# One RWKV-7 layer with a gated ConvFFN: own buffers for the first raw weight block of each seven-product pair, stores and half of the sum of squares off GpSimd

## The chip, the cores and the metric

The kernel runs on one core of a Trainium2 chip. The metric is the device time of one execution in microseconds (us). Engines are named as the profile names them: PE is TensorE (PEld its weight loads), DVE VectorE, ACT ScalarE, POOL GpSimd, SP the engine that issues most of the DMAs (SPq in the rows).

## The reference, cut to what matters

One layer on 512 tokens (T) of width D = 2048, all float32: an RWKV-7 time mixer, then a ConvFFN with 5504 hidden channels; each between two RMS norms and scaled by a conditioning vector. What the change touches is the residual between the two halves, and the ConvFFN's up-projection:

```
def _rms(x, g):
    y = xf * lax.rsqrt(jnp.mean(xf * xf, axis=-1, keepdims=True) + RMS_EPS)
    return (y * g).astype(x.dtype)
def _conv_ffn(h, w_in, conv_w, conv_b, w_out):
    u = _causal_dwconv(h @ w_in, conv_w, conv_b)
    gate, val = jnp.split(u, 2, axis=-1)
    return (jax.nn.silu(gate) * val) @ w_out
...
        x = x + g_m * _rms(y, norm_mix_post[layer])
        h = _rms(x, norm_ffn_pre[layer]) * (1 + sc_f) + sh_f
        f = _conv_ffn(h, ffn_w_in[layer], ffn_conv_w[layer], ffn_conv_b[layer], ffn_w_out[layer])
```

Each output of `_rms` needs the sum of squares over all 2048 channels of a token before it can be scaled.

## The kernel before, in words

Channels lie on the 128 partitions, tokens along the free axis; KT = 16 blocks of channels make up D, FT = 43 blocks the hidden width. Float32 accuracy comes from three products of rounded parts: a weight tile is split into wh (rounded, a cast on ACT, L220, L1314, L1304) and wl (the remainder, a subtraction on DVE, L222, L1315, L1305), the activations into xh and xl, and PE adds wh·xh + wh·xl + wl·xh. So a weight chunk of eight 128 x 128 tiles (512 KB, one DMA into a tile named wr) needs ACT and DVE work before PE can use it.

The stages that the change touches follow each other:

1. The output projection `wo` of the mixer. Blocks 0 to 9 are computed for all 512 tokens, blocks 10 to 15 for each half of the tokens (256 columns) in turn. `block_out` stores a block into yo and adds its squares into acc1. Beside it `ada_jobs` forms the modulation vectors on DVE (L482) from loads named js.
2. `between(h)` for half h of the tokens, a generator whose steps are laid among the matmuls: the scale from acc1, then for each of 16 blocks y = y·gm·rs (L1128) plus x (L1129, x in tiles xt), a store of y to DRAM for later (L1130, issued by POOL), its square (ACT, L1135) and the addition into accx (POOL, L1136). When all 16 are added, PE sums accx over the partitions with a matrix of ones (L1107), and each block is scaled (POOL, L1146; ACT, L1147) and split into xh (L1150) and xl (L1151), the input h2 of the ConvFFN. PE runs half 1 of `wo` beside `between(0)` and the first up-projection products of half 0 beside `between(1)`.
3. The up-projection `fi`. Hidden blocks 0 to 3 are done directly. For blocks 4 to 42 (39 of them, the list JS) gate and value block of the same number make a *pair*, which is computed with a seven-product scheme (Strassen's, in the form with few additions): the 2 x 2 grid is channels in two halves by tokens in two halves against four weight chunks, and 7 products of 8 tiles x 3 matmuls of 256 columns stand in place of 8. That is 168 matmuls a pair.

What a pair j loads (L1269, L1278, L1279): the chunks 0, 1 and 3 as raw blocks, l11, l12 and l22, and two sums in a tile ss, each a plain load by SP and an accumulating DMA issued by POOL. DVE makes two further sums, s2 = ss + l11 (`f_s2`, L1285) and s4 = s2 + l12 (`f_s4`, L1288), both in one tile s24. `f_split(n)` turns product n's weights (n = 7j + i) into halves wh/wl (four buffers each), or for every third n into one tile wx. Products 0, 4, 5 and 6 use h2 (xh, xl), products 1 to 3 the sums t2, t1, t3 of its quarters. PE's results are gathered by ACT and DVE (p1, u2, u3) into cg and cv (L1374, L1382, L1392), from which `hidden` makes the convolution (L1181 to L1183), the SiLU and the product ug·uv (POOL, L1195), stored by POOL (L1196).

The raw blocks l11, l12, l22 share the tag wr, three buffers in all, with one pair's three blocks in them:

```
    def f_raw(d, j, i):
        if j in JS:
            d[j] = wp.tile([P, CH * P], F32, tag="wr", name="wr", bufs=3)
            nc.sync.dma_start(d[j], chunk(j, i))
```

so each block is loaded into the buffer of the same block of the pair before, once that has been read for the last time. A tile pool hands out buffers by tag and adds the waits. The order in which each engine takes its instructions is not that of the source: a scheduler sets it when the program is built, from its own estimates of durations; each engine then runs its list strictly in order, SP's list of DMAs included.

Of the kernel before, what the change touches and what calls it, by code (L numbers as in the profile page):

```python
# [15 lines left out]
T = 512  # L16
# [138 lines left out]
def body(ctx, tc, g, ap):  # L155
# [289 lines left out]
    def all_of(*vis):  # L445
        return [(vi, q) for vi in vis for q in range(D // QC)]
# [635 lines left out]
    def spare(tag, name, w=T):  # L1082
        return ap_.tile([P, w], F32, tag=tag, name=name)

    big = [ap_.tile([P, KT // 4, T], F32, tag=f"y{i}", name="yo") for i in range(4)]

    xts = []
    gm, sf = (cp.tile([P, KT], F32, name=n) for n in ("gm", "sf"))
    gf = None
    V.tensor_scalar(sf, mods[4], 1.0, None, ALU.add)  # L1090
    V.tensor_tensor(sf, sf, vec[:, VI["fpre"], :], ALU.mult)
    yo = [big[b // (KT // 4)][:, b % (KT // 4)] for b in range(KT)]
    acc1, accx = spare("cg0", "acc1"), spare("cg1", "accx")
    NX = 4
    sqs = [spare(f"sq{i}", "osq") for i in range(2)]

    def block_out(b, ps, acc, dst, sq, cs=ALL, scale=1.0):
        S.activation(dst[:, cs], ps[:, cs], AF.Copy, scale=scale)
# [3 lines left out]
            S.activation(sq[:, cs], ps[:, cs], AF.Square)  # L1102
            V.tensor_tensor(acc[:, cs], acc[:, cs], sq[:, cs], ALU.add)

    def rstd_to(r, acc, b, cs):
        ps = bank(b)
        PE.matmul(ps[:, cs], ones, acc[:, cs], start=True, stop=True)  # L1107
        S.activation(r[:, cs], ps[:, cs], AF.Ln, bias=eps_r, scale=1.0 / D)
        S.activation(r[:, cs], r[:, cs], AF.Exp, scale=-0.5)  # L1109

# [3 lines left out]
    def between(h):  # L1114

        cs = HS[h]
        if not xts:
            xts.extend(spare(f"x{i}", "xt") for i in range(NX))
        for kt in range(min(NX - 1, KT)):
            nc.sync.dma_start(xts[kt % NX][:, cs], ap["xT"][kt, :, cs])  # L1120
        rstd_to(rs2, acc1, 7, cs)
        for _ in range(10):
            yield
        for kt in range(KT):
            if kt + NX - 1 < KT:
                nc.sync.dma_start(xts[(kt + NX - 1) % NX][:, cs], ap["xT"][kt + NX - 1, :, cs])
            y = yo[kt][:, cs]
            V.scalar_tensor_tensor(y, y, gm[:, kt:kt + 1], rs2[:, cs], ALU.mult, ALU.mult)  # L1128
            V.tensor_tensor(y, y, xts[kt % NX][:, cs], ALU.add)  # L1129
            G.dma_start(d_x1[kt][:, cs], y)  # L1130
            if kt == 0:
                S.activation(accx[:, cs], y, AF.Square)
            else:
                sq = sqs[kt % 2][:, cs]
                S.activation(sq, y, AF.Square)  # L1135
                G.tensor_tensor(accx[:, cs], accx[:, cs], sq, ALU.add)  # L1136
            for _ in range(2 + h):
                yield
        rstd_to(rs3, accx, 7, cs)
        for _ in range(4):  # L1140
            yield
        for kt in range(KT):
            while h == 0 and used[0] < kt:
                yield
            t, u = ap_.tile([P, TW], F32, tag="ht", name="ht", bufs=2), yo[kt][:, cs]
            G.tensor_tensor(t, u, rs3[:, cs], ALU.mult)  # L1146
            S.activation(u, t, AF.Identity, bias=mods[3][:, kt:kt + 1], scale=sf[:, kt:kt + 1])  # L1147
            if h == 0:
                h2[kt] = hslot()
            S.copy(h2[kt][0][:, cs], u)  # L1150
            V.tensor_tensor(h2[kt][1][:, cs], u, h2[kt][0][:, cs].bitcast(F32), ALU.subtract)  # L1151
            made[h] += 1
            yield

    for b in range(KT - NL):
        ps = po[b] if b < n0 else kinner("wo", b, yx, bank((2, 6)[b % 2]))
        block_out(b, ps, acc1, yo[b], sqs[b % 2])
        if b == 1:
            jobs = ada_jobs(ap_, all_of(2, 3)[on_pool:], 7, (2,), NX, get=lambda i: spare(f"x{i}", "js"), last=True, to="cv0")
            sides.append(jobs)  # L1160
    halves = [between(0), between(1)]
    drain(jobs)
    rs2, rs3 = spare("cv0", "rs2"), spare("cv1", "rs3")
    V.tensor_tensor(gm, mods[2], vec[:, VI["npost"], :], ALU.mult)
    for h in range(2):
        for i in range(NL):
# [9 lines left out]

    act = [None] * FT

    def conv(ps, c, tag, name):
        u = spare(tag, name)  # L1180
        S.activation(u, ps, AF.Identity, bias=fvec[:, 3, c:c + 1], scale=fvec[:, 2, c:c + 1])  # L1181
        V.scalar_tensor_tensor(u[:, 1:T], ps[:, 0:T - 1], fvec[:, 1, c:c + 1], u[:, 1:T], ALU.mult, ALU.add)  # L1182
        V.scalar_tensor_tensor(u[:, 2:T], ps[:, 0:T - 2], fvec[:, 0, c:c + 1], u[:, 2:T], ALU.mult, ALU.add)  # L1183
        return u

    def hidden(j, pg, pv):
        ug = conv(pg, j, f"x{j % 2}", "ug")
        silu = S.activation(ug, ug, AF.Silu)
        uv = conv(pv, FT + j, "x2", "uv")
        kept = {FT - 3: "xh", FT - 2: "xl"}.get(j)  # L1190
        if kept:
            act[j] = xp.tile([P, T], F32, tag=kept, name="act", bufs=XB)
# [72 lines left out]

    def f_raw(d, j, i):
        if j in JS:
            d[j] = wp.tile([P, CH * P], F32, tag="wr", name="wr", bufs=3)
            nc.sync.dma_start(d[j], chunk(j, i))  # L1269

    def f_sums(j):
# [79 lines left out]
    for m, j in enumerate(JS):  # L1351
# [1 line left out]
        A, B, C = (bank(order[(nb + i) % 7])[:, 0:TW] for i in range(3))  # L1353
        nb += 3
        if not tmp:
            tmp.extend(ap_.tile([P, 2, TW], F32, tag=t, name=n) for t, n in (("sq0", "p1"), ("sq1", "u2"), ("x3", "u3")))
        p1, u2, u3 = (t[:, m % 2] for t in tmp)
        cg, cv = (ap_.tile([P, T], F32, tag=f"{t}{m % 2}", name=t) for t in ("cg", "cv"))
        f_sums(j + 1)
        product(n, A, True, False)  # L1360
        S.copy(p1, A)
# [45 lines left out]
    def last(h, b):  # L1407

        cs = HS[h]
        rstd_to(rs4, acc2, b, cs)  # L1410
        for _ in range(10):
            yield
        xts, of, prev = [], [G if h and kt % 4 == 3 else V for kt in range(KT)], {}
# [131 lines left out]
```

## Time and profile before

| | us |
|---|---|
| median of 3 runs | 2808.62 |
| the three runs | 2794.98, 2808.62, 2809.04 |
| the profiled execution | 2797.79 |
| its span, first to last instruction | 2796.0 |
| PE busy | 2602.2 (93%) |
| DVE busy | 2057.6 (74%) |
| ACT busy | 1323.3 (47%) |
| POOL busy | 840.9 (30%) |
| mean granted PE clock | 0.977 of full |

The page lists busy time by engine, then the chain of waits that ended last, then groups of instructions by source line. Matmuls are pipelined: a matmul of 256 columns is shown 0.28 us long, but the next begins 0.12 us after it, so the time that PE needs is read from the distance between starts and not from the busy time of one. PEclk is the TensorE clock that was granted, in parts of full speed (2.4 GHz; the other level is 1.2 GHz).

### The profile page before, as it was taken

The page shows a single profiled execution, that of the slowest core. Times are in us where ns is not written, and L with a number is a line of the kernel's source. Part 1 is how long each engine was busy: PE and PEld are TensorE (multiplying, and loading weights), DVE is VectorE, ACT ScalarE, POOL GpSimd, SP SyncE. Part 2 cuts the span into 40 slices and gives each one's busy share as a digit, 9 for nine tenths or more (in the row PEclk, how much of TensorE's full clock was granted, in tenths as well). Part 3 has the DMA queues.
Part 4 walks back from the last instruction along what each step waited for, and adds up shares of the span by engine and source line. Part 5 has one row for each costly group of instructions (what it writes and reads, how often), then busy time and mean ns, then how long its engine had stood idle before and what let it go on. Part 6 is the DMA issues. An engine that isn't in the chain of part 4 may idle for free.

```text
span 2796.0 us, 47774 instructions
## 1 busy us (share of the span) xinstructions
PE 2602.2 (93%) x17754; PEld 2283.0 (82%) x17754; DVE 2057.6 (74%) x3103; ACT 1323.3 (47%) x2313; POOL 840.9 (30%) x925
## 2 busy tenths in 40 slices
PE   5899999989999999997899999999999999999997
PEld 3568787767777877796889999999999988888896
DVE  6978688888777687578887777777777776644377
ACT  4442355544454454435654445444444454343464
POOL 3643114677897355005521111111111210000000
PEclk9999999999999999998999999999999999999998
DMA  8759876667766675485576666666666648623266
GB/s 315 277 206 332 266 239 207 195 222 214 197 198 199 165 210 150 146 278 181 190 200 185 183 171 177 179 182 187 180 170 176 186 159 294 232 98 98 91 205 206
DMA packets 299338, 555.60 MB, mean 199 GB/s; under 512 B 124800, under 2 KB 153856, under 8 KB 295008
## 3 DMA queue, kind: packets, MB, share of 16 engines
q1 hardware_dynamic: 267776, 436.85, 49.2%
q0 software_dynamic: 30896, 114.97, 14.9%
q8 instruction: 140, 2.29, 0.3%
q14 instruction: 94, 0.77, 0.1%
q10 hardware_dynamic: 432, 0.72, 0.1%
HBM read 474.18 MB, written 78.25 MB: 198 GB/s over the span
## 4 chain that ended last, share of the span: by engine, by line
PE 32%; DMA 13%; DVE 9%; issue 5%; ACT 2%; POOL 0%; DVEq 0%; SPq 0%; ACTq 0%; POOLq 0%
DMA wr<-w 10%; PE bk L267 7%; PE bk L265 7%; PE bk L266 7%; PE bk L1330 4%; PE bk L1328 4%; PE bk L1329 4%; DVE wx L1305 2%; DMA js<-ada 2%; DVE wl L1315 1%; DVE wl L222 1%; DVE ja L482 1%; DVE uv L1183 1%; DVE yo L1128 0%; DVE ug L1182 0%
## 5 line engine op out<-in xcount | busy, mean ns | idle before, releaser
L265 PE MATMUL bk<-xh,wh 128*128 128x512 f32 (+1 forms) x2204 | 782.2, 364 | 17.5 <-ACT xh L1150 5.0
L266 PE MATMUL bk<-xl,wh 128*128 128x512 f32 (+1 forms) x2204 | 786.2, 360 | 6.3 <-DVE xl L1151 6.3
L267 PE MATMUL bk<-xh,wl 128*128 128x512 f32 (+1 forms) x2204 | 768.3, 361 | 13.4 <-DVE wl L222 12.5
L220 ACT CAST wh<-wr 128x512 fp32r<-128x512 f32 x584 | 356.3, 619 | 525.4 <-PE bk L266 432.4
L222 DVE TENSOR_TENSOR wl<-wr,wh 128x512 fp32r<-128x512 f32 x518 | 386.4, 754 | 201.2 <-ACT wh L220 182.9
L265 PEld LDWEIGHTS bk<-xh,wh 128*128 128x128 f32 x2204 | 421.2, 193 | 82.5 <-ACT xh L1150 6.1
L267 PEld LDWEIGHTS bk<-xh,wl 128*128 128x128 f32 x2204 | 412.0, 192 | 78.8 <-DVE wl L222 17.8
L266 PEld LDWEIGHTS bk<-xl,wh 128*128 128x128 f32 x2204 | 422.0, 191 | 65.8 <-DVE xl L1151 6.6
L1279 POOL DMA_DIRECT2D ss<-w x78 | 68.1, 873 | 689.6 <-DMA ss<-w 284.2
L1330 PE MATMUL bk<-xh,wl 128*128 128x256 f32 x832 | 237.5, 286 | 11.9 <-DVE wl L1315 11.9
L1328 PE MATMUL bk<-xh,wh 128*128 128x256 f32 x832 | 237.4, 285 | 3.8 <-DVE cv L1374 1.8
L1329 PE MATMUL bk<-xl,wh 128*128 128x256 f32 x832 | 236.4, 284 | 0.0
L1330 PEld LDWEIGHTS bk<-xh,wl 128*128 128x128 f32 x832 | 160.3, 193 | 14.6 <-DVE wl L1315 14.6
L482 DVE SCALAR_TENSOR_TENSOR ja<-js,cs,ja 128x512 f32<-128x512 f32 x165 | 123.6, 749 | 61.5 <-DMA js<-ada 60.5
L1328 PEld LDWEIGHTS bk<-xh,wh 128*128 128x128 f32 x832 | 160.4, 193 | 5.7 <-ACT wh L1314 3.4
L1329 PEld LDWEIGHTS bk<-xl,wh 128*128 128x128 f32 x832 | 160.4, 193 | 0.0
L1425 POOL TENSOR_TENSOR fo<-fo,rs 128x256 f32<-128x256 f32 x4 | 3.6, 912 | 490.0 <-ACT rs L1109 490.0
L1315 DVE TENSOR_TENSOR wl<-wr,wh 128x512 fp32r<-128x512 f32 x156 | 129.3, 853 | 1.3 <-ACT wh L1314 1.1
L222 POOL TENSOR_TENSOR wl<-wr,wh 128x512 fp32r<-128x512 f32 x66 | 99.0, 1503 | 95.0 <-ACT wh L220 75.1
L1330 PE MATMUL bk<-xh,wx 128*128 128x256 f32 x416 | 118.6, 285 | 0.7 <-DVE wx L1305 0.5
L1328 PE MATMUL bk<-xh,wx 128*128 128x256 f32 x416 | 118.0, 284 | 0.0
L1329 PE MATMUL bk<-xl,wx 128*128 128x256 f32 x416 | 117.9, 283 | 0.0
(298 smaller groups left out, 5936.2 us busy)
## 6 DMA issues: line engine op xcount, KB each, us to landing
wr<-w SPq DMA_DIRECT2D x409, 512.0 KB
js<-ada SPq DMA_DIRECT2D x256, 256.0 KB
ss<-w SPq DMA_DIRECT2D x78, 512.0 KB
ss<-w POOLq DMA_DIRECT2D x78, 512.0 KB, 9.2
ada<-ada SPq DMA_DIRECT2D x32, 1024.0 KB
d_bnd<-bnd POOLq DMA_DIRECT2D x16, 768.0 KB, 3.9
d_gs<-big POOLq DMA_DIRECT2D x16, 768.0 KB, 4.7
d_act<-ug POOLq DMA_DIRECT2D x41, 256.0 KB, 9.7
```

The costliest lines, as they stand in the source:

```text
L220: S.copy(hi, r)
L222: ins = on.tensor_tensor(lo, r, hi.bitcast(F32), ALU.subtract)
L265: PE.matmul(out[:, cs], wh[0:kp, 0:m], xh[0:kp, cs], start=start, stop=False)
L266: PE.matmul(out[:, cs], wh[0:kp, 0:m], xl[0:kp, cs], start=False, stop=False)
L267: PE.matmul(out[:, cs], wl[0:kp, 0:m], xh[0:kp, cs], start=False, stop=stop)
L482: eng.scalar_tensor_tensor(a, w, c, a, ALU.mult, ALU.add)
L1279: G.dma_start(t[:, i], chunk(j, other), accum_op=ALU.add)
L1305: V.tensor_tensor(lo, src, hi.bitcast(F32), ALU.subtract)
L1315: wst["last"] = V.tensor_tensor(lo, r, hi.bitcast(F32), ALU.subtract)
L1328: PE.matmul(ps, wh, xh, start=start and k == 0, stop=False, skip_group_check=True)
L1329: PE.matmul(ps, wh, xl, start=False, stop=False, skip_group_check=True)
L1330: PE.matmul(ps, wl, xh, start=False, stop=k == CH - 1, skip_group_check=True)
```

## The change

Four things, all in the stages above:

- The first raw block l11 of a pair leaves the tag wr and gets two buffers of its own (tags b0 and b1, taken in turn by j). l12 and l22 keep the three wr buffers for themselves.
- In `between`, the store of y is issued by SP and no longer by POOL. The squares of even blocks are added into accx on POOL as before, those of odd blocks into acc1 on DVE; the matrix of ones sums both.
- x is fetched into six tiles and no longer four; `ada_jobs` uses the same six.
- To make room the small tiles are laid out anew, as six tags of two rows each (`pair`). p1, u2, u3, cg and cv, which had two buffers each, now have one.

```
-    def rstd_to(r, acc, b, cs):
+    def rstd_to(r, accs, b, cs):
         ps = bank(b)
-        PE.matmul(ps[:, cs], ones, acc[:, cs], start=True, stop=True)
+        for i, acc in enumerate(accs):
+            PE.matmul(ps[:, cs], ones, acc[:, cs], start=i == 0, stop=i == len(accs) - 1)
...
-            G.dma_start(d_x1[kt][:, cs], y)
-            if kt == 0:
-                S.activation(accx[:, cs], y, AF.Square)
+            nc.sync.dma_start(d_x1[kt][:, cs], y)
+            acc, on = ((accx, G), (acc1, V))[kt % 2]
+            if kt < 2:
+                S.activation(acc[:, cs], y, AF.Square)
             else:
                 sq = sqs[kt % 2][:, cs]
                 S.activation(sq, y, AF.Square)
-                G.tensor_tensor(accx[:, cs], accx[:, cs], sq, ALU.add)
+                on.tensor_tensor(acc[:, cs], acc[:, cs], sq, ALU.add)
...
     def f_raw(d, j, i):
         if j in JS:
-            d[j] = wp.tile([P, CH * P], F32, tag="wr", name="wr", bufs=3)
+            d[j] = (wp.tile([P, CH * P], F32, tag="wr", name="wr", bufs=3) if i else
+                    ap_.tile([P, CH * P], F32, tag=f"b{j % 2}", name="w11"))
             nc.sync.dma_start(d[j], chunk(j, i))
...
         if not tmp:
-            tmp.extend(ap_.tile([P, 2, TW], F32, tag=t, name=n) for t, n in (("sq0", "p1"), ("sq1", "u2"), ("x3", "u3")))
-        p1, u2, u3 = (t[:, m % 2] for t in tmp)
-        cg, cv = (ap_.tile([P, T], F32, tag=f"{t}{m % 2}", name=t) for t in ("cg", "cv"))
+            t = ap_.tile([P, 3, TW], F32, tag="b4", name="p1")
+            tmp.extend([[t[:, i] for i in range(3)], pair("b5", "cg")])
+        (p1, u2, u3), (cg, cv) = tmp
```

The scheduler answers with other lists. On SP, early in the pair stage, before: wr_14451 is l11 of the second pair, wr_14547, wr_14610 and wr_14698 are l12 and l22 of that pair and l11 of the third; ss is the sums of the pair after next.

```order
L1269 DMA wr_14451<-w 128x1024
L1278 DMA ss_14357<-w 128x1024 x2
L1269 DMA wr_14547<-w 128x1024
L1269 DMA wr_14610<-w 128x1024
L1269 DMA wr_14698<-w 128x1024
L1278 DMA ss_14397<-w 128x1024 x2
L1269 DMA wr_14794<-w 128x1024
```

The same place on SP now: wr_14308 and wr_14486 are l22 of the first and l12 of the second pair, w11_14633 l11 of the third; wr_14549, wr_14729 and w11_14870 the same one pair on.

```order
L1277 DMA wr_14308<-w 128x1024
L1277 DMA wr_14486<-w 128x1024
L1277 DMA w11_14633<-w 128x1024
L1286 DMA ss_14299<-w 128x1024 x2
L1277 DMA wr_14549<-w 128x1024
L1277 DMA wr_14729<-w 128x1024
L1277 DMA w11_14870<-w 128x1024
L1286 DMA ss_14336<-w 128x1024 x2
```

The loads l12 and l11 moved one pair ahead relative to the sums: before, l11 of the third pair stands behind the third pair's sums; now that place holds l11 of the fourth.

On DVE, before, in the second pair: the last splits that read wr_14451 (l11 of this pair), and the sum s2 of the third pair, which reads wr_14698 (l11 of the third, loaded into the buffer that wr_14451 had).

```order
L1315 TENSOR_TENSOR wl_14576<-wr_14451,wh_14575 128x512
L1315 TENSOR_TENSOR wl_14580<-wr_14451,wh_14579 128x512
L1382 TENSOR_TENSOR cv_14396<-bk6_14390,p1_14392 128x256
L1305 TENSOR_TENSOR wx_14386<-s24_14376,wx_14386 128x1024
L1182 SCALAR_TENSOR_TENSOR uv_14692<-cv_14396,fvec_68,uv_14692 128x511
L1315 TENSOR_TENSOR wl_14638<-ss_14397,wh_14637 128x512
L1285 TENSOR_TENSOR s24_14376<-ss_14357,wr_14698 128x1024
```

The same place on DVE now: w11_14390 is l11 of the second pair, w11_14633 that of the third, in the buffer that the first pair's had.

```order
L1323 TENSOR_TENSOR wl_14515<-w11_14390,wh_14514 128x512
L1323 TENSOR_TENSOR wl_14519<-w11_14390,wh_14518 128x512
L1390 TENSOR_TENSOR cg_14335<-bk6_14332,p1_14334 128x256
L1313 TENSOR_TENSOR wx_14328<-s24_14318,wx_14328 128x1024
L1187 SCALAR_TENSOR_TENSOR uv_14136<-cg_14335,fvec_68,uv_14136 128x511
L1323 TENSOR_TENSOR wl_14577<-ss_14336,wh_14576 128x512
L1293 TENSOR_TENSOR s24_14318<-ss_14299,w11_14633 128x1024
```

DVE's list is the same here; what moved is which load the last row reads, and since when its buffer has been free.

On DVE at the hand-over from `wo` to `fi` (the first xl), before: L1128 and L1129 are the second half of `between`, L1151 makes xl of the first half, yo_11519 to yo_11522 are the four quarters of the channels.

```order
L1103 TENSOR_TENSOR acc1_11527<-acc1_11527,osq_11530 128x256
L1128 SCALAR_TENSOR_TENSOR yo_11519<-yo_11519,gm_11523,rs2_12070 128x256 x4
L1128 SCALAR_TENSOR_TENSOR yo_11520<-yo_11520,gm_11523,rs2_12070 128x256 x4
L1129 TENSOR_TENSOR yo_11519<-yo_11519,xt_12515 128x256
L1128 SCALAR_TENSOR_TENSOR yo_11521<-yo_11521,gm_11523,rs2_12070 128x256 x3
L1151 TENSOR_TENSOR xl_12826<-yo_11519,xh_12825 128x256
L1128 SCALAR_TENSOR_TENSOR yo_11521<-yo_11521,gm_11523,rs2_12070 128x256
```

The same place on DVE now (L1155 makes xl, L1131 is the scaling of the second half).

```order
L1155 TENSOR_TENSOR xl_12774<-yo_11519,xh_12773 128x256
L222 TENSOR_TENSOR wl_13119<-wr_13011,wh_13118 128x512
L1155 TENSOR_TENSOR xl_12944<-yo_11519,xh_12943 128x256
L222 TENSOR_TENSOR wl_13144<-wr_13011,wh_13143 128x512
L1107 TENSOR_TENSOR acc_11527<-acc_11527,osq_11531 128x256
L1155 TENSOR_TENSOR xl_12954<-yo_11519,xh_12953 128x256
L1155 TENSOR_TENSOR xl_12964<-yo_11519,xh_12963 128x256
```

The first xl moved ahead of the second half's scaling; before, twelve instructions of the second half stand ahead of the first xl.

## Rows read from the trace of the kernel before

**Rows 1.** The page, chain that ended last: its shares by line

```profile
DMA wr<-w 10%; PE bk L267 7%; PE bk L265 7%; PE bk L266 7%; PE bk L1330 4%; PE bk L1328 4%; PE bk L1329 4%; DVE wx L1305 2%; DMA js<-ada 2%; DVE wl L1315 1%; DVE wl L222 1%; DVE ja L482 1%; DVE uv L1183 1%; DVE yo L1128 0%; DVE ug L1182 0%
```

**Rows 2.** Stretches: length, busy PE, PEld, DVE, ACT, POOL (instructions), PEclk, DMA share, GB/s

```profile
1260.00:1404.00 144.00, 115.33 (x851) 109.47 (x849) 123.51 (x182) 87.78 (x188) 75.77 (x96) 0.89 0.59 186
...
1428.60:2284.70 856.10, 808.75 (x6554) 798.78 (x6554) 646.53 (x889) 409.93 (x654) 142.91 (x152) 0.99 0.64 176
```

**Rows 3.** Waits of PE, 1428.6 to 2284.7: total us, times, longest

```profile
PE bk L1330 <- DVE wx L1305: 28.0, 14, 3.6
PE bk L1330 <- DVE wl L1315: 12.6, 15, 1.1
```

**Rows 4.** Waits of DVE, 1428.6 to 2284.7

```profile
DVE s L1285 <- DMA wr<-w: 82.8, 37, 4.4
DVE s L1288 <- DMA wr<-w: 70.8, 28, 4.4
DVE wx L1305 <- ACT wx L1304: 19.5, 25, 2.6
```

**Rows 5.** Timeline from 1603.70: start, length, instruction [idle before, releaser]

```profile
1603.70 1.22 DVE L1305 TENSOR_TENSOR wx<-wr,wx 128x1024 fp32r<-128x1024 f32 x1
...
1604.95 0.33 SPq L1269 DMA_DIRECT2D wr<-w  x1
...
1609.31 1.23 DVE L1285 TENSOR_TENSOR s<-ss,wr 128x1024 f32<-128x1024 f32 x1 [1.16 <-DMA wr<-w]
```

**Rows 6.** Timeline of DVE, the next pair

```profile
1623.77 0.68 DVE L1315 TENSOR_TENSOR wl<-wr,wh 128x512 fp32r<-128x512 f32 x1
...
1631.65 1.22 DVE L1285 TENSOR_TENSOR s<-ss,wr 128x1024 f32<-128x1024 f32 x1 [3.80 <-DMA wr<-w]
```

**Rows 7.** Timeline of PE, 1608 to 1618

```profile
1608.07 0.28 PE L1328 MATMUL bk<-t2h,wh 128*128 128x256 f32 x1
1608.19 0.28 PE L1329 MATMUL bk<-t2l,wh 128*128 128x256 f32 x1
...
1615.80 0.38 PE L1330 MATMUL bk<-xh,wl 128*128 128x256 f32 x1 [1.09 <-DVE wl L1315]
...
1617.49 0.42 PE L1329 MATMUL bk<-t3l,wx 128*128 128x256 f32 x1
1617.70 0.42 PE L1330 MATMUL bk<-t3h,wx 128*128 128x256 f32 x1
```

**Rows 8.** Timeline of DVE, 1613 to 1622: last read of cg, next write of cv

```profile
1613.26 0.75 DVE L1183 SCALAR_TENSOR_TENSOR ug<-cg,fvec,ug 128x510 f32<-128x510 f32 x1
...
1622.12 0.42 DVE L1374 TENSOR_TENSOR cv<-u,bk 128x256 f32<-128x256 f32 x1
```

**Rows 9.** Timeline of PE at the hand-over from wo to fi

```profile
1302.55 1.22 PE L1107 MATMUL bk<-accx,ones 128*128 128x256 f32 x2 [5.14 <-POOL accx L1136]
...
1307.70 1.65 PE L265 MATMUL bk<-xh,wh 128*128 128x256 f32 x6 [2.14 <-ACT xh L1150]
1315.63 0.58 PE L266 MATMUL bk<-xl,wh 128*128 128x256 f32 x1 [6.29 <-DVE xl L1151]
```

**Rows 10.** Timeline of DVE around the hand-over

```profile
1270.02 0.42 DVE L1129 TENSOR_TENSOR yo<-yo,xt 128x256 f32<-128x256 f32 x1
...
1284.43 1.43 DVE L1129 TENSOR_TENSOR yo<-yo,xt 128x256 f32<-128x256 f32 x1
...
1306.89 5.41 DVE L1128 SCALAR_TENSOR_TENSOR yo<-yo,gm,rs 128x256 f32<-128x256 f32 x8 [6.58 <-ACT rs L1109]
```

**Rows 11.** Timeline of POOL, 1284

```profile
1284.83 0.74 POOL L1136 TENSOR_TENSOR accx<-accx,osq 128x256 f32<-128x256 f32 x1
```

**Rows 12.** Groups by line, 1262 to 1404: count, busy, mean ns, idle before

```profile
L1136 POOL TENSOR_TENSOR accx<-accx,osq 128x256 f32<-128x256 f32 x30 | 26.9, 896 | 9.7 <-ACT osq L1135 8.5
L1130 POOL DMA_DIRECT2D d_x<-yo x32 | 17.8, 557 | 161.6 <-ACT wh L220 141.8 <-DVE yo L1129 14.2 <-ACT osq L1135 4.3
L1129 DVE TENSOR_TENSOR yo<-yo,xt 128x256 f32<-128x256 f32 x32 | 18.4, 587 | 1.2 <-DMA xt<-xT 1.1
```

More of the change, by code (lines that the diff above doesn't have):

```diff
@@ L1085, in body, with pair @@
     big = [ap_.tile([P, KT // 4, T], F32, tag=f"y{i}", name="yo") for i in range(4)]
-    xts = []
+    def pair(tag, name):
+        t = ap_.tile([P, 2, T], F32, tag=tag, name=name)
+        return [t[:, 0], t[:, 1]]
     gm, sf = (cp.tile([P, KT], F32, name=n) for n in ("gm", "sf"))
@@ L1092, in body @@
     yo = [big[b // (KT // 4)][:, b % (KT // 4)] for b in range(KT)]
-    acc1, accx = spare("cg0", "acc1"), spare("cg1", "accx")
-    NX = 4
-    sqs = [spare(f"sq{i}", "osq") for i in range(2)]
+    acc1, accx = pair("b0", "acc")
+    xts = pair("b2", "xt") + pair("b3", "xt") + pair("b5", "xt")
+    NX = len(xts)
+    sqs = pair("b4", "osq")
     def block_out(b, ps, acc, dst, sq, cs=ALL, scale=1.0):
@@ L1116, in between @@
         cs = HS[h]
-        if not xts:
-            xts.extend(spare(f"x{i}", "xt") for i in range(NX))
         for kt in range(min(NX - 1, KT)):
             nc.sync.dma_start(xts[kt % NX][:, cs], ap["xT"][kt, :, cs])
-        rstd_to(rs2, acc1, 7, cs)
+        rstd_to(rs2, (acc1,), 7, cs)
         for _ in range(10):
@@ L1135, in between @@
                 S.activation(sq, y, AF.Square)
-                G.tensor_tensor(accx[:, cs], accx[:, cs], sq, ALU.add)
+                on.tensor_tensor(acc[:, cs], acc[:, cs], sq, ALU.add)
             for _ in range(2 + h):
                 yield
-        rstd_to(rs3, accx, 7, cs)
+        rstd_to(rs3, (accx, acc1), 7, cs)
         for _ in range(4):
@@ L1158, in body @@
         if b == 1:
-            jobs = ada_jobs(ap_, all_of(2, 3)[on_pool:], 7, (2,), NX, get=lambda i: spare(f"x{i}", "js"), last=True, to="cv0")
+            jobs = ada_jobs(ap_, all_of(2, 3)[on_pool:], 7, (2,), NX, get=lambda i: xts[i], last=True, to="b1")
             sides.append(jobs)
@@ L1162, in body @@
     drain(jobs)
-    rs2, rs3 = spare("cv0", "rs2"), spare("cv1", "rs3")
+    rs2, rs3 = pair("b1", "rs")
     V.tensor_tensor(gm, mods[2], vec[:, VI["npost"], :], ALU.mult)
@@ L1177, in body, with conv @@
     act = [None] * FT
-    def conv(ps, c, tag, name):
-        u = spare(tag, name)
+    units = {}
+    def conv(ps, c, u):
         S.activation(u, ps, AF.Identity, bias=fvec[:, 3, c:c + 1], scale=fvec[:, 2, c:c + 1])
@@ L1186, in hidden @@
     def hidden(j, pg, pv):
-        ug = conv(pg, j, f"x{j % 2}", "ug")
+        if not units:
+            units["g"], units["v"] = pair("b2", "ug"), spare("b3", "uv")
+        ug = conv(pg, j, units["g"][j % 2])
         silu = S.activation(ug, ug, AF.Silu)
-        uv = conv(pv, FT + j, "x2", "uv")
+        uv = conv(pv, FT + j, units["v"])
         kept = {FT - 3: "xh", FT - 2: "xl"}.get(j)
@@ L1409, in last @@
         cs = HS[h]
-        rstd_to(rs4, acc2, b, cs)
+        rstd_to(rs4, (acc2,), b, cs)
         for _ in range(10):
```

## The prediction

> **What bounds the kernel now.** I read the chain of waits first. Beside PE's own lines its largest share is a DMA, the load of raw weight chunks, with 10% [rows 1]. That is odd for a kernel whose PE is busy 93% of the span, so I cut the span into stretches, and asked in each who waits for whom.
>
> The largest stretch that the change touches is the pair stage, 856.1 us long [rows 2]. It holds 39 pairs x 168 = 6552 matmuls of 256 columns. Undisturbed, they start 0.12 us apart [rows 7], so PE needs 6552 x 0.12 = 786.2 us, and the stage loses 69.9 us. Of this PE stands idle for 856.1 - 808.75 = 47.3 us. The other 22.6 us are matmuls at the slower level of the clock: after the stall that ends at 1615.80 starts are 0.21 us apart and no longer 0.12 [rows 7], which is the 1.2 GHz level, and the granted clock of the stage is 0.99.
>
> PE waits for remainders made on DVE (wx 28.0, wl 12.6 us) [rows 3]. DVE is busy for 646.5 of the 856.1 us [rows 2], so it isn't full. It stands still for raw loads: 82.8 us ahead of the sum s2 and 70.8 us ahead of s4 [rows 4], 153.6 us in all or 3.9 us a pair. DVE runs in order, so every split behind such a sum is late with it.
>
> Why the load is late stands in the timeline. At 1603.70 DVE splits l11 for the last time, until 1604.92; SP issues the load of the next l11 into that buffer at 1604.95; the sum that reads it starts at 1609.31, 4.36 us after the issue, having waited 1.16 us [rows 5]. In the next pair the split ends at 1624.45, the sum starts at 1631.65, and 3.80 us of that was idle [rows 6]. In the list the sum stands five rows behind the split. So the buffer is the bound: freed, filled and read within a fifth of a pair.
>
> **The change part by part.**
>
> *l11 in two buffers.* Its load now goes into the buffer that was freed one whole pair earlier; at 20 to 22 us a pair that is some 20 us ahead of the sum, against 4.4 to 7.2 us that such loads take (above). l12 and l22 rotate through three buffers, so l12 goes where the l22 before last was, freed more than a pair ahead of s4. SP's list is in order: l22, l12, l11, sums. Each of these waits for a split of the pair before, none for one that comes later than its reader, so none holds up the next beyond that. I therefore count both waits, 153.6 us, as gone on DVE. What does PE get of it? At most the 69.9 us. At least nothing, if the waits only took up DVE's slack. DVE's work, 646.5 us, fits into 786 us with 140 us to spare; the other wait of size, wx for ACT's cast, is 19.5 us [rows 4]. I take 62 us, 8 us short of all, since splits come in bursts and some short stalls with a few slow matmuls will stay. New loads per pair are the same; the DMA share goes from 0.64 to 0.64 x 856/794 = 0.69.
>
> Here the Trainium skill has a figure: "DMA: Bandwidth & Descriptors", in "Anatomy of one DMA — SWDGE (gpsimd) path", gives about 2.0 us of fixed cost, and "Where 436 GB/s comes from" the rate; by these I estimate 2.0 + 1.2 = 3.2 us for 512 KB. The trace has 4.36 and 7.2 us from issue to use, so the page would make each wait shorter than the rows show; by it the waits would come to about 154 - 39 x 2 x 1.2 = 60 us, and PE's part, scaled alike, to 27 us instead of 62. The rows decide.
>
> *cg, cv, p1, u2, u3 in one buffer.* The convolution's last read of cg ends at 1614.01, the next pair's first write of cv starts at 1622.12 [rows 8]: 8.1 us of room, filled by products. I count 0, and 39 us for each us by which the reads come later than that.
>
> *Stores on SP, half of the additions on DVE.* POOL loses 32 issues of 0.557 us, 17.8 us, and 16 of 30 additions of 0.896 us, 14.3 us [rows 12]. SP gains 32 issues at 0.33 us [rows 5], 10.6 us, each waiting for its y with weight loads behind it; in SP's list the loads stand behind stores whose y precedes, on DVE, the split that frees the load's buffer, so I count 0, and up to 6 us (two chunks of 24 matmuls x 0.12) if that cover fails. DVE gains 14 additions of 0.42 us, as L1129 of the same shape takes undisturbed [rows 10]: 5.9 us. Against this, L1129 took 1.43 us beside a POOL addition [rows 10, 11], and 0.587 us in the mean [rows 12]; with 16 POOL additions gone, up to 16 x 0.48 = 7.7 us of stretching may go, if each stretches one DVE instruction by half the 1.01 us excess seen there. So DVE's work changes by +5.9 to -1.8 us; I take +2.
>
> On that the Trainium skill says, in "SBUF — State Buffer", section "SBUF: two separate sides", that a DVE instruction with two SBUF inputs and a GpSimd one lock each other out for whole instructions. By it the stretch would be a POOL addition's whole 0.74 us, 16 x 0.74 = 11.8 us less, and DVE's work 5.9 us smaller and not 2 larger. The row, 1.43 against 0.42 us, agrees with the rule; no row shows it for every addition.
>
> *The hand-over.* PE waits 5.14 us for the sum of squares, 2.14 for xh, 6.29 for xl [rows 9], 13.6 us in all, and the granted clock over these 144 us is 0.89 [rows 2]. The xl is late as DVE has first to scale the second half (8 scalings in 5.41 us after an idle 6.58) [rows 10]. Now POOL's chain is half as long, and the first xl stand ahead of that scaling. But DVE is busy for 123.5 of the 144 us [rows 2], and the work that went first is only put off. So at most 144 - 123.5 - 2 = 18.5 us, at least 0; I take 10.
>
> *Six tiles for x and js.* Loads start earlier beside matmuls that fill PE; I count 0.
>
> **Sum.** -62 - 10 = -72 us on the profiled execution's 2797.8, so 2725.8 us. The three runs lie at 2795.0, 2808.6 and 2809.0, so the median is 10.8 us above the profiled one; which of the two the changed kernel will fall on isn't told by the trace, and I add 4: **2730 us**.
>
> **The rivals.**
>
> *A: DVE's list is the bound, not the loads.* PE's waits are for wx and wl, and the sums stand at the same places as before, in bursts of splits and convolutions. For it: DVE would be 646.5/794 = 81% busy. Against it: the idle time on DVE is all of it named, and three quarters of it are loads. If half the loss stays: -35 - 10, with the 4, 2757 us.
>
> *B: the hand-over costs instead of gaining.* DVE is the fuller engine there. +5.9 us of additions and 6 us of weights behind stores, 12 in all: -62 + 12 + 4, 2752 us.
>
> *C: the change doesn't do what it says.* SP is one queue: w11 stands behind two loads that wait for splits, and if those hold the queue until the old moment, the sum waits as before. Against it: both wait for splits that lie most of a pair ahead. Then nothing but the hand-over moves: 2798 to 2809 us.
>
> *D: slower, by the single cg and cv.* Place: the convolution's reads on ACT and DVE, ahead of the next pair's first write into the same tile. Without the loads' waits PE and DVE run closer together, and a read that is late by more than the 8.1 us stops DVE, and with it the splits. Price: 39 us per us. It ends more than 0.5% slower from (72 + 14)/39 = 2.2 us beyond the room; at 3 us it is 2730 + 117 = 2847 us. For it: ACT waits for cg and cv between its casts. Against it: the reads would have to slip by half a pair.
>
> **How the numbers follow.** A change under 0.5%, 14 us, can't be told from none here. My forecast has 0.68, A 0.14, B 0.06, C 0.07, D 0.05. The first three are faster: 0.88; C is the same: 0.07; D slower: 0.05. Range: low, all of the loss and all of the hand-over's bound gone, 2797.8 - 69.9 - 18.5 = 2709; high, half of the pair stage, nothing at the hand-over, and the upper of the two run levels, 2797.8 - 35 + 10.8 = 2774.
>
> **What would show it.** In the changed profile: DVE's waits for w11 and wr ahead of s2 and s4 under 20 us in all; the pair stage 790 to 800 us long with PE idle under 10 us and a granted clock of 1.00; l11 issued 15 us or more ahead of its sum; PE's waits for accx and xl at the hand-over under 5 us together, and DVE over 90% busy in the stretch of `between`. I am wrong if DVE still waits over 75 us for raw loads (C), if it doesn't and PE still stands idle for over 25 us behind wx and wl (A), if SP's weight loads come late behind stores (B), or if ACT or DVE wait ahead of a write into cg or p1 (D).

## The result, and the profile after

The changed kernel takes 2733.57 us (median of 4 runs, 2732.37 to 2739.32), the kernel before 2808.83 (4 runs, 2794.98 to 2814.33); the ratio is 0.9737, 95% interval 0.9701 to 0.9773. The forecast was 2730 us, between 2709 and 2774.

The profiled execution after took 2739.32 us, with a span of 2737.6. The chain of waits, by line, has lost its largest share that was not PE's. What is left of the load of raw weight chunks is the "DMA wr<-w 0%" near the end, where [rows 1] had 10%:

```profile
PE bk L1338 10%; PE bk L1337 10%; PE bk L1336 10%; PE bk L267 8%; PE bk L265 8%; PE bk L266 7%; DVE wl L222 1%; DMA js<-ada 1%; DMA x1t<-d_x 1%; DMA out<-x1t 1%; DVE yo L1131 0%; DMA wr<-w 0%; PE bk L859 0%; DVE xl L1155 0%; PE bk L464 0%
```

I cut both spans at two matmuls that both kernels have: the first ones-matmul of the hand-over (before it everything is the mixer and most of wo), and the first of the pair stage. The columns are those of [rows 2]. The first line is the hand-over of the kernel before, the other two are the hand-over and the pair stage of the changed kernel:

```profile
1261.93:1428.64 166.71, 137.36 (x935) 127.38 (x934) 143.00 (x213) 104.49 (x217) 82.22 (x103) 0.90 0.62 194
```

```profile
1277.63:1441.17 163.54, 137.76 (x940) 128.56 (x938) 138.29 (x231) 103.84 (x220) 61.73 (x56) 0.94 0.64 202
1441.17:2227.40 786.23, 786.23 (x6553) 786.23 (x6552) 650.03 (x885) 418.03 (x652) 137.63 (x150) 1.00 0.70 190
```

| stretch | before, us | after, us | difference |
|---|---|---|---|
| up to the hand-over | 1261.9 | 1277.6 | +15.7 |
| hand-over | 166.7 | 163.5 | -3.2 |
| pair stage | 856.0 | 786.2 | -69.8 |
| behind it | 511.3 | 510.2 | -1.1 |
| span | 2796.0 | 2737.6 | -58.4 |

The pair stage now is its matmuls and nothing else: PE is busy for all of the 786.23 us, at a granted clock of 1.00, where it had 808.75 busy of 856.10 and 0.99 [rows 2]. 6552 matmuls 0.12 us apart are 786.2 us.

PE has no wait left there. DVE's are these (us in total, times, longest); neither sum waits for a load, where s2 and s4 waited 82.8 and 70.8 us [rows 4]:

```profile
DVE wx L1313 <- ACT wx L1312: 61.1, 64, 2.6
DVE p L1381 <- PE bk L1338: 36.6, 39, 2.5
DVE wl L1323 <- ACT wh L1322: 14.8, 22, 0.9
DVE cg L1390 <- PE bk L1338: 11.9, 13, 1.6
```

DVE's slack of 136 us is still there. It has only moved to places where nobody waits for DVE: behind ACT's casts, and ahead of PE's results.

The timelines of SP and DVE show the load that [rows 5, 6] follow (start, length, instruction). It is issued at 1619.55; the sum that reads it starts at 1643.45, 23.9 us later where it was 4.36, with no idle time ahead of it. One instruction of SP, one of DVE:

```profile
1619.55 0.33 SPq L1277 DMA_DIRECT2D w<-w  x1
```

```profile
1643.45 1.22 DVE L1293 TENSOR_TENSOR s<-ss,w 128x1024 f32<-128x1024 f32 x1
```

At the hand-over the three waits of [rows 9], for the sum of squares, xh and xl, are gone. One of 2.88 us for xh is left, ahead of the second half, where the kernel before has one too. Others have grown in their place. PE's waits there, in the kernel before and in the changed one:

```profile
PE bk L267 <- DVE wl L222: 8.1, 12, 2.3
PE bk L1107 <- POOL accx L1136: 6.7, 2, 5.1
PE bk L266 <- DVE xl L1151: 6.3, 1, 6.3
PE bk L265 <- ACT xh L1150: 5.0, 2, 2.9
PE bk L265 <- ACT wh L220: 2.6, 1, 2.6
PE bk L1107 <- ACT rs L1108: 0.6, 1, 0.6
```

```profile
PE bk L267 <- DVE wl L222: 13.8, 11, 4.9
PE bk L265 <- ACT wh L220: 8.9, 4, 3.6
PE bk L265 <- ACT xh L1154: 2.9, 1, 2.9
```

So 18.6 us of waits (sum 6.7, xl 6.3, xh 5.0, rs 0.6) became 2.9, and 10.7 us of waits for split weights became 22.7. The net is 3.7 us of 29.3.

### The profile page after: what moved, and what is told of

The parts are those of the page before. It is cut to its first block, busy times and chain, and to the rows that moved or that the text cites. A ratio compares the mean times of both kernels' runs of the same rounds, so it can differ in the third digit from the quotient of the medians.

```text
span 2737.6 us, 47712 instructions
## 1 busy us (share of the span) xinstructions
PE 2593.3 (95%) x17758; PEld 2279.8 (83%) x17758; DVE 2051.9 (75%) x3117; ACT 1332.1 (49%) x2313; POOL 812.1 (30%) x877
## 4 chain that ended last, share of the span: by engine, by line
PE 53%; DVE 4%; DMA 3%; issue 1%; ACT 0%; POOL 0%; SPq 0%; DVEq 0%; ACTq 0%; POOLq 0%
PE bk L1338 10%; PE bk L1337 10%; PE bk L1336 10%; PE bk L267 8%; PE bk L265 8%; PE bk L266 7%; DVE wl L222 1%; DMA js<-ada 1%; DMA x1t<-d_x 1%; DMA out<-x1t 1%; DVE yo L1131 0%; DMA wr<-w 0%; PE bk L859 0%; DVE xl L1155 0%; PE bk L464 0%
## 5 line engine op out<-in xcount | busy, mean ns | idle before, releaser
L222 DVE TENSOR_TENSOR wl<-wr,wh 128x512 fp32r<-128x512 f32 x518 | 383.0, 746 | 215.4 <-ACT wh L220 195.0
L482 DVE SCALAR_TENSOR_TENSOR ja<-js,cs,ja 128x512 f32<-128x512 f32 x120 | 90.0, 750 | 49.4 <-DMA js<-ada 48.9
L1474 DVE TENSOR_TENSOR xl<-act,xh 128x512 fp32r<-128x512 f32 (+1 forms) x172 | 92.7, 555 | 28.4 <-ACT xh L1473 28.4
```

The lines of the kernel that those rows point to most:

```text
L222: ins = on.tensor_tensor(lo, r, hi.bitcast(F32), ALU.subtract)
L482: eng.scalar_tensor_tensor(a, w, c, a, ALU.mult, ALU.add)
L1474: V.tensor_tensor(ahl[e][1][:, cs], act[f][:, cs], ahl[e][0][:, cs].bitcast(F32), ALU.subtract)
```

## The experiments

A single trace of this kernel says little about its total, since the stretch ahead of the hand-over differs between executions by more than most of these edits (last experiment). So I read each stage from the trace, cut as above, and give the total beside it.

**l11 back among the shared buffers.**

```diff
-            d[j] = (wp.tile([P, CH * P], F32, tag="wr", name="wr", bufs=3) if i else
-                    ap_.tile([P, CH * P], F32, tag=f"b{j % 2}", name="w11"))
+            d[j] = wp.tile([P, CH * P], F32, tag="wr", name="wr", bufs=3)
```

> The changed kernel, but l11 goes back among the three shared raw buffers; the single cg, cv and p1, the stores on SP, the halved sums and the order of the program stay. Theory (the load that goes into the buffer just freed is what held DVE up): DVE waits for raw loads ahead of s2 and s4 come back, 130 to 170 us together, the pair stage takes 848 to 864 us instead of 786, and the time is 2733.6 + 70 = about 2803 us (2790 to 2812). Rival (the gain came from the order on SP or from the other edits): the pair stage stays under 800 us and the time under 2750 us.

Measured: 2797.59 us (2790.04 to 2802.76), ratio to the kernel before 0.9972 [0.9951, 0.9993]; the pair stage takes 850.3 us. DVE's waits for raw loads are back, 147.5 us:

```profile
DVE s L1292 <- DMA wr<-w: 74.4, 37, 4.1
DVE s L1295 <- DMA wr<-w: 73.1, 29, 4.9
```

The theory holds: with l11 among the shared buffers again, all the other edits together bring 0.1 to 0.5%. The edit takes two things back, though: l11's second buffer, and with it the third buffer that l12 and l22 had to rotate through.

**One buffer of its own for l11, three for l12 and l22**

```diff
-                    ap_.tile([P, CH * P], F32, tag=f"b{j % 2}", name="w11"))
+                    ap_.tile([P, CH * P], F32, tag=f"b0", name="w11"))
```

> The changed kernel, but l11 has one buffer of its own instead of two, so that its load again goes into the buffer of its predecessor; l12 and l22 still rotate through three. Theory (each wait costs its share): the waits ahead of s2 come back, about 80 us, those ahead of s4 stay under 10 us; the pair stage loses 80/154 of 70 us, 36 us, and the time is about 2770 us (2755 to 2785). Rival 1 (the two waits stand in for each other, what one does not take the other does): 2795 to 2805 us. Rival 2 (DVE's slack of about 3 us a pair hides one wait alone): under 2745 us.

Measured: 2786.81 us (2775.41 to 2792.84), pair stage 843.5 us. DVE's first wait, in the same view:

```profile
DVE s L1293 <- DMA w<-w: 119.1, 37, 5.4
```

The wait ahead of s4 is gone, yet the one ahead of s2 has grown from 82.8 to 119.1 us. So the stage loses 57 us and not 36. The median lies 2 us above the theory's range and below rival 1's, but the growing wait is rival 1's mechanism: what one wait no longer takes, the other does, in part. Of the 64.1 us between l11_back (850.3) and the changed kernel (786.2), the third buffer for l12 and l22 brings 6.8 alone, no more than what two traces of the kernel before differ by (last experiment), and l11's second buffer on top of it 57.3.

**One fixed buffer each for l12 and l22, two for l11**

```diff
                     ap_.tile([P, CH * P], F32, tag=f"b{j % 2}", name="w11"))
+            if i == 3:
+                wp.tile([P, CH * P], F32, tag="wr", name="wr", bufs=3)
```

> The changed kernel, but l12 and l22 have one fixed buffer each (a third tile of the rotation is taken and never filled); l11 keeps its two. Theory (each wait costs its share): the waits ahead of s4 come back, about 70 us, those ahead of s2 stay under 10 us; the pair stage loses 71/154 of 70 us, 32 us, and the time is about 2766 us (2750 to 2780). Rival 1 (the waits stand in for each other): 2795 to 2805 us. Rival 2 (DVE's slack hides one wait alone): under 2745 us.

Measured: 2732.91 us (2731.28 to 2742.34), and a pair stage like the changed kernel's:

```profile
1433.96:2220.19 786.23, 786.23 (x6554) 786.23 (x6552) 650.19 (x886) 418.29 (x652) 137.64 (x150) 1.00 0.69 190
```

This run does not test what it was meant to test. The extra tile is never written, and it takes no buffer. SP still loads three blocks of l12 and l22 ahead of the first matmul of the stage, at 1433.96, when none of them has been read to the end; one fixed buffer for each leaves room for two. SP's timeline here, and in the changed kernel, whose stage begins at 1441.17:

```profile
1415.61 12.55 SPq L1279 DMA_DIRECT2D wr<-w  x3
```

```profile
1422.85 12.03 SPq L1277 DMA_DIRECT2D wr<-w  x3
```

The program built from this edit has the instructions of the changed kernel, in the same order on each engine and at the same addresses. So neither my theory nor a rival is decided. What the run gives is a second trace of the changed kernel and four more times. Whether l12 and l22 need their third buffer once l11 has two stays open. The timelines speak for some need: in the changed kernel DVE's last split of an l12 ends 6.5 us ahead of the next pair's s4 (median of 38), while in the kernel before a load of l12 that s4 waited for took 8.1 us from its issue (median of 28). By these I estimate that with a single buffer some of the wait ahead of s4 would come back; what it would cost PE no run shows.

**More work for DVE in the pair stage**

```diff
             V.tensor_tensor(s24[0][:, 0], ss[j % 2][:, 0], l11[j], ALU.add)
+            V.tensor_tensor(s24[0][:, 0], ss[j % 2][:, 0], l11[j], ALU.add)
...
         V.tensor_tensor(s24[0][:, 1], s24[0][:, 0], l12[j], ALU.add)
+        V.tensor_tensor(s24[0][:, 1], s24[0][:, 0], l12[j], ALU.add)
```

> The changed kernel, but the sums s2 and s4 of every pair are made twice on DVE (the second one writes the same values again): 78 more instructions of 1.22 us, 95 us, so that DVE is busy for 745 of the pair stage's 786 us instead of 650. Theory (DVE's slack is real, the loads were the only thing that held PE up): the pair stage stays under 792 us and the time under 2740 us. Rival (rival A of the prediction: DVE works in bursts, and what is left of its list is nearly the bound): PE waits for wx and wl again, the pair stage takes 805 to 830 us, and the time is 2752 to 2780 us.

Measured: 2740.59 us (2737.26 to 2745.12). The pair stage:

```profile
1441.57:2230.22 788.65, 788.09 (x6553) 786.80 (x6552) 714.80 (x962) 420.43 (x652) 143.22 (x150) 1.00 0.69 189
```

PE stays within 2.4 us of its matmuls, and its only listed wait is 0.2 us. The theory holds for the stage; the total misses its bound by 0.6 us, and the hand-over of this execution was 2.7 us longer than in the changed kernel's. DVE is busy for 64.8 us more and not 95, though the 77 instructions that the trace has more last 1.22 us each. In part other work got shorter: the 104 half splits of l12 and l22 took 0.86 us each in the mean, against 1.06 in the changed kernel, those of s2 and s4 0.79 against 0.69. The rest I did not settle. Rival A, DVE's list as the bound, is refuted up to this dose.

**Both edits of the hand-over undone**

```diff
-            nc.sync.dma_start(d_x1[kt][:, cs], y)
-            acc, on = ((accx, G), (acc1, V))[kt % 2]
-            if kt < 2:
+            G.dma_start(d_x1[kt][:, cs], y)
+            acc, on = accx, G
+            if kt < 1:
...
-        rstd_to(rs3, (accx, acc1), 7, cs)
+        rstd_to(rs3, (accx,), 7, cs)
```

> The changed kernel with the pair stage as it is, but at the hand-over both edits undone: the x1 stores are issued by GpSimd again, and all 30 additions of the sum of squares are GpSimd's. From the first ones-matmul of the hand-over to the first matmul of the pair stage the traces of the kernel before show 166.7 and 166.5 us, those with the changed hand-over 163.5, 164.1, 163.2 and 160.2 us. Theory from these (the edits are worth about 4 us): 164 to 170 us there, and the time is 2733 + 4 = 2737 us (2730 to 2744). Rival (the 10 us of the prediction, hidden by a difference between executions): 171 us or more there, 2743 us or more.

Measured: 2737.64 us (2730.62 to 2747.88); hand-over 168.4 us. PE's waits there are the old ones again:

```profile
PE bk L267 <- DVE wl L222: 9.7, 13, 2.0
PE bk L266 <- DVE xl L1155: 7.1, 1, 7.1
PE bk L1112 <- POOL acc L1140: 5.3, 2, 4.1
PE bk L265 <- ACT xh L1154: 5.2, 2, 2.9
PE bk L265 <- ACT wh L220: 2.7, 2, 1.9
PE bk L1112 <- ACT rs L1113: 0.6, 1, 0.6
```

That is the theory's range. Together the two edits are worth 2 to 8 us of hand-over, this one trace against the five with the changed hand-over (160.2 to 166.2).

**Only the stores undone; only the additions undone, twice.** The edits are the first changed line of the diff above, or the rest of it.

> The changed kernel, but the x1 stores are issued by GpSimd again; the additions stay halved. Theory (stores on SP hold weight loads up: in the changed kernel PE waits 22.7 us for wl and wh of the hand-over where it waited 10.7 us before): the weights come earlier, PE's waits for wl and wh fall under 14 us, the hand-over takes 150 to 159 us instead of 163, and the time is 2722 to 2731 us. Rival (the weights are late because DVE's list is full of scalings and additions there, whoever issues the stores; GpSimd's issues of 0.56 us lengthen its additions' chain): 162 to 168 us there, 2732 to 2740 us.

> The changed kernel, but all 30 additions of the sum of squares are on GpSimd again; the stores stay on SP. Theory (GpSimd's chain of additions sets when the second rstd comes, and an addition there can take 3 us beside DVE): PE waits 4 us or more for the sum again, the hand-over takes 165 to 172 us, and the time is 2735 to 2743 us. Rival (DVE is the fuller engine, so 14 additions of 0.42 us less on it bring the splits earlier by 5.9 us): 155 to 161 us there, 2725 to 2731 us.

> The same kernel as sums_back once more (stores on SP, all 30 additions on GpSimd), for a second trace and more times: its hand-over took 151.9 us in one trace, that of the changed kernel's code 160.2 to 166.2 us in five. Theory (one of the two edits is enough to take GpSimd's chain off PE's path, and the second one only loads DVE): 149 to 157 us again, no wait of PE for the sum over 1 us, and a time 4 to 10 us under the changed kernel's. Rival (spread between executions): 158 us or more.

Measured: with the stores back on GpSimd 2729.91 us (2723.02 to 2733.62) and 155.3 us at the hand-over; with all additions back on GpSimd 2727.54 (2719.53 to 2732.96) and 151.9, and once more 2727.99 (2722.48 to 2731.93) and 155.6, as sums_again's theory said. For the additions the theory of sums_back falls: PE does not wait for the sum again. Its waits at the hand-over, first trace:

```profile
PE bk L267 <- DVE wl L222: 11.6, 16, 2.5
PE bk L265 <- ACT wh L220: 5.0, 3, 2.3
PE bk L265 <- ACT xh L1154: 0.9, 1, 0.9
```

For the stores the hand-over came out where the theory put it, at 155.3 us, but its reason, that the weights come earlier, is not borne out: PE still waits 16.7 us for wl and wh, not under 14, and ACT's waits for raw weight chunks at the hand-over are no shorter with the stores back. These waits in the kernel before, in the changed one, and with the stores back:

```profile
ACT wh L220 <- DMA wr<-w: 21.0, 12, 4.9
```

```profile
ACT wh L220 <- DMA wr<-w: 17.3, 11, 7.6
```

```profile
ACT wh L220 <- DMA wr<-w: 23.3, 15, 4.1
```

Either edit alone takes GpSimd's chain off PE's path. The second one then brings nothing there; with both, and six x tiles, the hand-over is longer (160.2 to 166.2 us in five traces). In which queue or list that cost arises is not shown.

**A fourth raw weight buffer, with four x tiles; the four x tiles alone; the fourth buffer with the additions back**

```diff
-        r = wp.tile([P, CH * P], F32, tag="wr", name="wr", bufs=3)
+        r = (wst["more"].tile([P, CH * P], F32, tag="b5", name="w4") if "more" in wst and c % 4 == 0 else
+             wp.tile([P, CH * P], F32, tag="wr", name="wr", bufs=3))
...
-        while wst["load"] < min(wst["end"], h // 2 + 3):
+        while wst["load"] < min(wst["end"], h // 2 + 3 + ("more" in wst)):
...
-    xts = pair("b2", "xt") + pair("b3", "xt") + pair("b5", "xt")
+    xts = pair("b2", "xt") + pair("b3", "xt")
...
+    wst["more"] = ap_
...
+    wst.pop("more")
     JS = list(range(NF + NP, FT))
```

> The changed kernel, but at the hand-over and in the direct blocks behind it every fourth weight chunk goes into a fourth raw buffer, the one that held two of the six x tiles (x and js have four again), and chunks are loaded one further ahead. Theory (PE's 22.7 us of waits for wl and wh at the hand-over are weight loads that start too late, as in the pair stage): those waits fall under 12 us, and the hand-over takes 148 to 158 us instead of 160 to 166. Rival (the splits are late because DVE's and ACT's lists are full there, the raw chunks lie ready): the waits stay at 18 us or more, and the hand-over takes 160 us or more.

> The changed kernel with four tiles instead of six for x and js, and nothing else: what raw_four gives up for its buffer. The prediction counts the two more tiles at nothing: hand-over 160 to 166 us, time within 6 us of the changed kernel's. Rival (x comes late with four): DVE waits for x over 3 us, and the hand-over takes 168 us or more.

> sums_back and raw_four together (stores on SP, all additions on GpSimd, a fourth raw weight buffer, four tiles for x). Theory (late loads and DVE's list are two costs): 143 to 151 us at the hand-over, 2715 to 2725 us. Rival (the pair stage's first two pairs give the gain back, as they gave back 6 of sums_back's 11 us): hand-over and pair stage together 944 us or more, as in sums_back, and 2726 us or more.

Measured: the fourth buffer 2731.51 us (2719.78 to 2735.11), the four tiles alone 2731.16 (2725.51 to 2733.20), the buffer with the additions back 2731.65 (2716.32 to 2744.15). With the buffer PE's waits for split weights are half of the changed kernel's (its lines stand one lower, L223 is the split):

```profile
PE bk L268 <- DVE wl L223: 10.4, 11, 2.7
PE bk L1113 <- DVE acc L1108: 2.7, 1, 2.7
PE bk L1113 <- POOL acc L1141: 1.1, 1, 1.1
PE bk L266 <- ACT wh L221: 1.0, 1, 1.0
```

That is 11.4 us of waits instead of 22.7, and a hand-over of 151.1 us, as theory said. But the edit has the four x tiles in it, and these alone have 17.9 us of waits and 155.8 us. So the buffer's own part is 6.5 us of waits and 4.7 us of hand-over, and ACT's waits for raw chunks fall from 21.2 us to 4.3: the late weights are late loads in part. With the additions back too the hand-over is 148.6 us, in the range of sums_raw4's theory; hand-over and pair stage are 940.6, under its rival's 944, but the time is the rival's. It is not the way to a faster kernel, as all traces side by side show (the waits are PE's at the hand-over, the clock is the granted one there, and the last column adds hand-over and pair stage):

| kernel | hand-over | for wl, wh | for sum, xh, xl, rs | clock there | pair stage | both |
|---|---|---|---|---|---|---|
| before | 166.7 | 10.7 | 18.6 | 0.90 | 856.0 | 1022.8 |
| both edits undone | 168.4 | 12.4 | 18.2 | 0.90 | 786.3 | 954.7 |
| changed | 163.5 | 22.7 | 2.9 | 0.94 | 786.2 | 949.8 |
| stores back | 155.3 | 16.7 | 5.5 | 0.98 | 789.9 | 945.2 |
| additions back | 151.9 | 16.6 | 0.9 | 0.96 | 792.3 | 944.2 |
| additions back, again | 155.6 | 20.3 | 1.7 | 0.97 | 789.5 | 945.1 |
| four x tiles | 155.8 | 17.9 | 4.3 | 0.98 | 787.4 | 943.2 |
| fourth raw buffer | 151.1 | 11.4 | 5.4 | 0.95 | 792.1 | 943.2 |
| both, buffer and additions back | 148.6 | 12.6 | 4.3 | 0.98 | 792.0 | 940.6 |

The waits are not all of the difference. Of the 7.7 us between the hand-overs of the changed kernel and of the four x tiles 3.4 are waits; PE runs 940 and 939 instructions there and is busy for 137.8 and 133.2 us, at a granted clock of 0.94 and 0.98. And the second trace of the changed kernel, that of l12_two, has the same 25.6 us of waits and takes 160.2 us, at 0.97. So some 3 to 4 us between two rows of this table can be the clock's, with the waits alike.

What is gained at the hand-over is in part given back at the head of the pair stage, whose first splits are then late. PE's first two stalls there, with the additions back (start, length, instruction, idle time before it and its releaser):

```profile
1433.58 0.39 PE L1338 MATMUL bk<-xh,wl 128*128 128x256 f32 x1 [2.35 <-DVE wl L1323]
1436.30 0.58 PE L1338 MATMUL bk<-t2h,wl 128*128 128x256 f32 x1 [0.51 <-DVE wl L1323]
```

No total of the five kernels below the changed one is separated from its 0.9737 [0.9701, 0.9773]; the best, with the additions back, has 0.9725 [0.9700, 0.9750] and 0.9723 [0.9695, 0.9750]. It may be some 6 us faster: its eleven times lie between 2719.53 and 2732.96 us, the eight of the changed kernel's program between 2731.28 and 2742.34. But they were taken at other times, between which the kernel before went from a median of 2804.6 to one of 2810.5, so that isn't shown. The four x tiles missed my own expectation (160 to 166): their 155.8 us lie outside the five traces with six, though that is one trace.

**The kernel before, a second time** (no edit)

> The kernel before, unchanged, for a second trace of it. In the changed kernel's trace the last group of one-column matmuls ahead of the hand-over starts at 1263.8 us, in the trace of before at 1248.1 us, 15.7 us earlier, though both run the same instructions up to there. Theory (spread between executions, the two traces lying at opposite ends of it): this execution starts that group 4 to 16 us later than the first one, 1252 to 1264 us. Rival (the changed memory layout slows the mixer): 1248 us within 2 us here, and 1262 us or more in every kernel with the changed layout.

Measured: 2801.42 us, the group starts at 1259.70 us, 11.6 us later than in the first trace. In the other kernels it starts between 1257.8 and 1267.7, 1250.3 with the fourth raw buffer. So the +15.7 us of the table above is spread between executions: the trace of before was an early one, that of the changed kernel a late one. The pair stage of this second trace took 849.4 us, its hand-over 166.5, so the gain in the pair stage is 63 to 70 us.

## Why the prediction was right, and where not

*The pair stage.* Forecast -62, measured -69.8. The mechanism was as told: the load is ahead by 23.9 us, DVE's waits are gone, PE is full. The 8 us kept back for "some short stalls" were too cautious, and the stage ended below the 790 to 800 us that I had asked of it.

*Both waits as gone*: right, with the buffers together. What the prediction could not tell is what each buffer is worth. The two waits were not two costs: with the s4 wait taken away alone, the one ahead of s2 grew to 119.1 us, and 57 of the 70 us stayed lost. Whether l11's second buffer alone would do is open, as l12_two did not test it. The side estimate by the Trainium skill ("DMA: Bandwidth & Descriptors", section "Anatomy of one DMA — SWDGE (gpsimd) path") used a figure for DMAs that GpSimd issues, and SP issues these loads. The 27 us worked out from it are 69.9 scaled; 62 scaled alike would be 24. Neither entered the sum.

*The single cg, cv, p1, u2, u3*, counted at 0: right. PE's stage is its matmuls, so no read comes late; rival D has nothing to stand on, and neither has C.

*The hand-over.* Forecast -10, measured -3.2 in the profile and about 3 in the mean of the five traces (163.4 against 166.6). The step that failed is "SP gains 32 issues ... so I count 0", and with it the 0 for six tiles. I had put 6 us to the stores if their cover failed, and gave that to rival B alone, with a chance of 0.06. The waits for split weights rose by 12.0 us; the table gives the additions on DVE, the stores on SP and, by one trace, the two more x tiles a part in it each. How each makes the weights late stays open: ACT waited less for raw chunks than before (17.3 and 21.0 us), and more for GpSimd's additions (7.7 and 3.7). Rival B named the late weights and the 12 us; they went against a gain of 15.7 us in PE's other waits, which it had left out.

*DVE's work at the hand-over*, where I took +2: it fell from 143.0 to 138.3 us, by 4.7, with 14 additions more (7.1 us). The scaled y's addition lasts 416 ns in the mean, down from the 587 of L1129 [rows 12]; the groups after:

```profile
L1131 DVE SCALAR_TENSOR_TENSOR yo<-yo,gm,rs 128x256 f32<-128x256 f32 x32 | 16.9, 585 | 0.1
L1132 DVE TENSOR_TENSOR yo<-yo,xt 128x256 f32<-128x256 f32 x32 | 12.3, 416 | 0.0
L1140 DVE TENSOR_TENSOR acc<-acc,osq 128x256 f32<-128x256 f32 x14 | 7.1, 504 | 2.8 <-ACT osq L1139 2.8
```

But moving the additions did not do that. With all 30 back on GpSimd DVE has 139.85 us of work with the stores on GpSimd too (first line), and 138.06 with the stores on SP (second line):

```profile
1281.52:1449.94 168.42, 137.96 (x936) 128.26 (x935) 139.85 (x214) 105.35 (x218) 88.86 (x104) 0.90 0.61 196
```

```profile
1277.48:1429.40 151.92, 134.34 (x935) 125.51 (x934) 138.06 (x208) 101.72 (x215) 71.60 (x70) 0.96 0.68 216
```

With the additions halved and the stores on the same engine, DVE has 139.30 and 138.29 us, 0.55 less and 0.23 more. So the edit's own net is near 0, inside my -1.8 to +5.9. The Trainium skill, "SBUF — State Buffer", section "SBUF: two separate sides", by which the sum was 5.9 us less, is further from these pairs. In [rows 10, 11] the stretch of 1.01 us is also more than the whole 0.74 us of the addition beside it, and half of it is 0.505 and not 0.48. What else took some 3 us off DVE's work since the first trace (141.3 us in the second of before) I did not find.

*The run level, and luck.* The +4 us stood for what the trace can't tell, and it was too small. From the hand-over on the changed trace is 74.1 us shorter; 2797.8 less these is 2723.7, and the median lies 9.9 us above that, much as the median of before lies 11.0 above its trace. The trace's own -58.4 differs from this by the 15.7 us ahead of the hand-over, which are spread. So three terms missed: the pair stage with what is behind it brought 8.9 us more, the hand-over 6.8 less, and the level came out 5.9 higher. These nearly cancel, and that the time came within 3.6 us of the forecast is luck. That it lies in the range at all rests on the pair stage, whose mechanism was right.

## What to carry to other kernels

When an in-order engine waits for loads at several places, look for the buffers that are freed just ahead of their reader, and count their waits together: taking the later wait away alone moved half of it to the earlier one, and 57 of the 70 us stayed lost. Two edits that relieve the same engine are not two gains: once it is off the critical path, the second brought nothing here and cost some us. An edit that is meant to take a buffer away has to be looked for in the trace before its time is read. And read a stage's gain between two instructions that both traces have; a total carries the spread of all that ran before.

## What the runs showed of the hardware

In the changed kernel's trace GpSimd's addition of 128 x 256 took between 0.72 and 3.55 us. The longest ran from 1337.41 to 1340.96, while DVE worked through a row of splits and differences without a gap; three that ran later, with DVE mostly waiting, took 0.72 each. But DVE at work does not always hold it up: one that began at 1341.49, with no gap on DVE either, took 0.73, and there DVE's scaling from 1341.50 took 1.01 us, where the one from 1343.70 took 0.48. The timeline of POOL in the changed kernel:

```profile
1337.41 3.55 POOL L1140 TENSOR_TENSOR acc<-acc,osq 128x256 f32<-128x256 f32 x1 [5.01 <-ACT osq L1139]
...
1349.76 3.19 POOL L1140 TENSOR_TENSOR acc<-acc,osq 128x256 f32<-128x256 f32 x1 [4.66 <-ACT osq L1139]
1353.48 0.72 POOL L1140 TENSOR_TENSOR acc<-acc,osq 128x256 f32<-128x256 f32 x1 [0.53 <-ACT osq L1139]
1354.73 0.72 POOL L1140 TENSOR_TENSOR acc<-acc,osq 128x256 f32<-128x256 f32 x1 [0.53 <-ACT osq L1139]
1355.98 0.72 POOL L1140 TENSOR_TENSOR acc<-acc,osq 128x256 f32<-128x256 f32 x1 [0.53 <-ACT osq L1139]
```

The mean rose from 896 ns [rows 12] to 1474, though GpSimd had half as many to do. I had looked only at DVE being held up by GpSimd. In these long additions it is the other way round, and ACT, whose casts of the next weights stand behind the squares in its list, waits 7.7 us in six of the squares for these additions.
